# Attention in a two-layer diffusion block: the values of two pairs of heads in one PSUM tile, and separate slot rings for probabilities and their transposes

## The chip, the cores and the metric

The kernel runs on one core of a Trainium2 chip. The metric is the device time of one execution in microseconds. In the profiles the engines are PE (TensorE, matrix products; PEld are its weight loads), DVE (VectorE), ACT (ScalarE), POOL (GpSimd) and SP (SyncE, which issues the DMAs here). `L814` is line 814 of the kernel.

## What is computed

Two layers over 256 latent and 256 context tokens of width 1024. Each layer normalizes and modulates its input, multiplies it by one wide input matrix, runs three mixers on parts of the result (a short convolution, a Fourier mixing, an attention), gates and sums them, projects the sum, and ends with a squared-ReLU network. The part that matters here is the attention, with 8 query heads of 64 channels in 2 groups, each group sharing one key and value head:

```python
def gqa(q, k, v):
    b, lq = q.shape[:2]
    qg = q.reshape(b, lq, N_KV_HEADS, GQA_GROUP, HEAD_DIM)
    s = jnp.einsum('bqgrd,bkgd->bgrqk', qg, k).astype(jnp.float32) * (HEAD_DIM ** -0.5)
    p = jax.nn.softmax(s, axis=-1).astype(v.dtype)
    o = jnp.einsum('bgrqk,bkgd->bqgrd', p, v)
    return o.reshape(b, lq, ATTN_WIDTH)
```

Latent queries (256) read 512 keys, those of the latents and of the context. Context queries (256) read the 256 context keys, and only in layer 0. All data are float32.

## The kernel before

**Precision.** Large products are made of three passes: each operand is split into a high and a low part (`hilo`, L445, for activations; `split`, L356, for weights), and `fm` (L411) issues high x high (L434), low x high (L437) and high x low (L439). The weight parts are made by one ACT cast (L359) and one DVE subtraction (L360) for each 1024 columns.

**Attention.** A unit is one head, one block of 128 queries, one stream (s = 0 latents, s = 1 context). Layer 0 has 32 units, layer 1 has 16 (latents alone). They stand in the order stream, i, query block, head, where head is i and then i + 4; so two units that follow each other are the two groups' heads of one pair, and four units are both query blocks of that pair. One unit has three steps:

- `softmax` (L783): two PE products of scores into a PSUM tile (L789), DVE's maximum (L792), ACT's exponential into a slot of a ring (L795), DVE's reciprocal and scaling (L797, L798).
- `flip` (L801): 4 PE transposes of the probabilities (2 for context units) into a PSUM tile (L804), and an ACT copy into another slot (L806).
- `values` (L809), once for two units: for each key block one product for each of the two groups (L814), whose 64 output rows go to one half of the partitions of a PSUM tile of 128 columns; then `hilo` writes the high part (ACT, L446) and the low part (DVE, L447) into `qT`, where the queries of these heads have been read.

Both probabilities and transposed probabilities take their slots from one ring of 8 slots of 512 columns (`ar`, L775) in the order of the calls. PSUM tiles of the attention come from a pool of 3 (`aux`, L83), as do a few others.

**What sets the order.** `attend` (L777) is a generator: each `yield` is one step. `fm` calls `attn.tick()` (L442) after each block of the contraction, and `Side` (L336) takes 1.3 steps per tick in layer 0 and 0.8 in layer 1 (`AR`, L36). The ticks are those of the gate products, `gates` (L845) and the two branch products (L869, L870): 20 ticks in each of four rounds (L857). What is left is taken by `attn.drain()` (L875) before the third gate (`agL`). The loop at L824 takes, for each n, `softmax` of unit n, `flip` of unit n - 2 and, when n is even, `values` of units n - 4 and n - 3. `mods` works in the same manner for the modulation vectors of later stages (L241 to L333): DVE accumulations, then four small products with `ones` (L283), an ACT copy of their result (L288) and two transposes (L293). The tile framework then orders the instructions of each engine by a simulated time line; semaphores make each instruction wait for its inputs and for its slot.

**Names.** `gateL` and `agL` are the stages of the two gate parts, with a tile's name behind: `gateL_mm` are the PSUM tiles of the gate products, `gateL_aux` those of the attention, `qkvL_big` the ring and also `qT`, `qkvL_vt` the values, `gateL_mod` the modulation products. A product of L814 is float32 and leaves two records in the trace, so 8 of them are 16 records.

## Time and profile before

| | |
|---|---|
| median of 3 runs | 1155.12 us (1152.49 to 1155.44) |
| the profiled execution | 1154.74 us, its span 1153.0 us |
| mean granted PE clock | 0.997 of full speed |
| products of L814 in the trace | 320 records, first at 157.5 us, last at 903.7 us |
| transposes of L804 | 160, each of 128 columns |
| score products of L789 | 96 |
| gate stage of layer 0 | 127.6 to 281.6 us |
| gate stage of layer 1 | 821.4 to 905.5 us |

PE's matmul records overlap: one starts while the one before is still draining. So the time that an instruction takes on PE is read from the start of one record to the start of the next, not from its duration. The time line merges equal instructions that follow each other; its columns are start and length in us, engine, line, operation, output and inputs, shape, and their number.

### The profile page before, as it was taken

How to read it: one execution, taken by the hardware profiler on the slowest of the kernel's cores; microseconds unless marked ns; L12 is line 12 of the kernel's file. 1: busy time of each engine (PE TensorE's matmuls, PEld its weight loads, DVE VectorE, ACT ScalarE, POOL GpSimd, SP SyncE). 2: the span in 40 equal slices, each digit the busy share in tenths (PEclk: the TensorE clock that was granted, in tenths of full speed). 3: DMA queues.
4: the chain of work that ended last, by engine and by line, in shares of the span. 5: the costliest groups of instructions: out<-in, count | busy, mean ns of one | idle time of the engine just before them, and what ended most of it. 6: DMA issues, size and time to landing. Idle time of an engine off the chain costs nothing.

```text
span 1153.0 us, 17815 instructions
## 1 busy us (share of the span) xinstructions
PE 1130.3 (98%) x7083; PEld 982.5 (85%) x7083; DVE 781.7 (68%) x1446; ACT 504.6 (44%) x896; POOL 59.2 (5%) x57
## 2 busy tenths in 40 slices
PE   6899999999999999999999999999999999999998
PEld 5689987887787998888888888899999999988986
DVE  4677775567879785776655664778876567756754
ACT  4244444434332354144235135245665446754652
POOL 2102100000000100000000000033300000000000
PEclk9999999999999999999999999999999999999999
DMA  9923222224556254556456664625434365556553
GB/s 290 289 80 107 92 92 89 84 86 124 186 164 198 77 170 141 170 180 198 129 166 218 201 198 149 202 77 170 142 113 144 111 201 183 183 176 190 183 183 110
DMA packets 156764, 180.03 MB, mean 156 GB/s; under 512 B 5228, under 2 KB 126472, under 8 KB 156680
## 3 DMA queue, kind: packets, MB, share of 16 engines
q1 hardware_dynamic: 156680, 178.88, 49.0%
q8 instruction: 56, 0.92, 0.3%
q14 instruction: 28, 0.23, 0.1%
HBM read 177.81 MB, written 1.05 MB: 155 GB/s over the span
## 4 chain that ended last, share of the span: by engine, by line
PE 88%; DMA 4%; SPq 3%; DVE 3%; ACT 1%; issue 1%; POOL 0%; DVEq 0%; ACTq 0%
PE ffL_mm L434 12%; PE ffL_mm L437 12%; PE ffL_mm L439 12%; PE gateL_mm L434 5%; PE gateL_mm L437 5%; PE gateL_mm L439 5%; PE ffL_mm L1064 3%; PE ffL_mm L1062 3%; PE ffL_mm L1063 3%; PE agL_mm L434 2%; PE agL_mm L437 2%; PE agL_mm L439 2%; SPq L465 2%; PE gateL_aux L814 2%; PE woL_mm L437 2%; PE woL_mm L439 2%
## 5 line engine op out<-in xcount | busy, mean ns | idle before, releaser
L359 ACT CAST ffL_whi<-ffL_raw 128x1024 fp32r<-128x1024 f32 x128 | 134.4, 1052 | 218.2 <-PE ffL_mm L439 164.3
L360 DVE TENSOR_TENSOR ffL_wlo<-ffL_raw,ffL_whi 128x1024 fp32r<-128x1024 f32 x127 | 155.1, 1222 | 99.1 <-ACT ffL_whi L359 99.0
L434 PE MATMUL ffL_mm<-woL_big,ffL_whi 128*128 128x258 f32 (+2 forms) x544 | 171.1, 329 | 0.0
L437 PE MATMUL ffL_mm<-woL_big,ffL_wlo 128*128 128x258 f32 (+2 forms) x544 | 170.5, 327 | 0.0
L439 PE MATMUL ffL_mm<-woL_big,ffL_whi 128*128 128x258 f32 (+2 forms) x544 | 133.2, 328 | 0.0
L434 PEld LDWEIGHTS ffL_mm<-woL_big,ffL_whi 128*128 128x128 f32 x544 | 103.0, 190 | 10.2 <-issue 1.6
L437 PEld LDWEIGHTS ffL_mm<-woL_big,ffL_wlo 128*128 128x128 f32 x544 | 103.2, 190 | 8.9 <-issue 0.4
L326 DVE SCALAR_TENSOR_TENSOR ffL_acc<-ffL_modr,cs,ffL_acc 128x512 f32<-128x512 f32 x126 | 90.4, 746 | 25.7 <-DMA ffL_modr<-in_w_mod_dram 24.6
L434 PE MATMUL ffL_mm<-ffL_big,ffL_whi 128*128 128x512 f32 (+1 forms) x288 | 105.3, 368 | 0.0
L437 PE MATMUL ffL_mm<-ffL_big,ffL_wlo 128*128 128x512 f32 (+1 forms) x288 | 104.9, 367 | 0.0
L439 PEld LDWEIGHTS ffL_mm<-woL_big,ffL_whi 128*128 128x128 f32 x544 | 91.0, 190 | 8.7
L439 PE MATMUL ffL_mm<-ffL_big,ffL_whi 128*128 128x512 f32 (+1 forms) x288 | 85.1, 367 | 0.0
L434 PEld LDWEIGHTS ffL_mm<-ffL_big,ffL_whi 128*128 128x128 f32 x288 | 54.3, 189 | 10.6 <-issue 2.1
L437 PEld LDWEIGHTS ffL_mm<-ffL_big,ffL_wlo 128*128 128x128 f32 x288 | 54.3, 189 | 9.0 <-issue 0.4
L439 PEld LDWEIGHTS ffL_mm<-ffL_big,ffL_whi 128*128 128x128 f32 x288 | 53.2, 189 | 8.7
L360 DVE TENSOR_TENSOR gateL_wlo<-gateL_raw,gateL_whi 128x1024 fp32r<-128x1024 f32 x40 | 48.8, 1221 | 13.5 <-ACT gateL_whi L359 13.3
L359 ACT CAST gateL_whi<-gateL_raw 128x1024 fp32r<-128x1024 f32 x40 | 42.0, 1050 | 26.7 <-PE gateL_mm L439 20.7
L792 DVE TENSOR_REDUCE gateL_mx<-gateL_aux 128x1 f32<-128x512 f32 (+1 forms) x48 | 28.7, 599 | 34.5 <-PE gateL_aux L789 34.2
L434 PE MATMUL gateL_mm<-n1L_big,gateL_whi 128*128 128x512 f32 x128 | 50.8, 398 | 0.0
L437 PE MATMUL gateL_mm<-n1L_big,gateL_wlo 128*128 128x512 f32 x128 | 50.8, 397 | 0.0
L1062 PE MATMUL ffL_mm<-ffL_whi,ffL_big 128*128 128x512 f32 x128 | 49.9, 390 | 0.0
L1063 PE MATMUL ffL_mm<-ffL_wlo,ffL_big 128*128 128x512 f32 x128 | 49.8, 389 | 0.0
(335 smaller groups left out, 2658.5 us busy)
## 6 DMA issues: line engine op xcount, KB each, us to landing
ffL_raw<-in_w_ff_dram SPq DMA_DIRECT2D x64, 1024.0 KB, 5.4
ffL_modr<-in_w_mod_dram SPq DMA_DIRECT2D x53, 512.0 KB, 5.8
gateL_raw<-in_w_in_dram SPq DMA_DIRECT2D x16, 1024.0 KB, 6.8
init_big<-in_w_mod_dram SPq DMA_DIRECT2D x16, 512.0 KB, 7.8
agL_raw<-in_w_in_dram SPq DMA_DIRECT2D x8, 1024.0 KB, 5.0
woL_raw<-in_w_o_dram SPq DMA_DIRECT2D x8, 1024.0 KB
qkvL_raw<-in_w_in_dram SPq DMA_DIRECT2D x6, 1024.0 KB
agL_modr<-in_w_mod_dram SPq DMA_DIRECT2D x11, 512.0 KB, 4.2
```

Of the source, the lines that this page charges most:

```text
L326: v = V.scalar_tensor_tensor(a, r[:, kk, :], w, a, op0=ALU.mult, op1=ALU.add)
L359: a = A.copy(hi[:, :n], src)
L360: b = eng.tensor_tensor(lo[:, :n], src, hi[:, :n].bitcast(F32), op=ALU.subtract)
L434: m = PE.matmul(d, wh, rh, start=kt == first, stop=False)
L437: PE.matmul(d, wl, rh, start=False, stop=False)
L439: PE.matmul(d, wh, rl, start=False, stop=kt == final)
L465: nc.sync.dma_start(t[:, f, i], w_mod[0, :, c0 : c0 + P].rearrange("(k p) n -> p k n", p=P))
L792: V.reduce_max(mx, sc, axis=AX.X, negate=True)
L814: PE.matmul(yp[g * HD : (g + 1) * HD, :], vt[:, k0 + kk, g * HD : (g + 1) * HD], pts[g][:, kk, :], start=kk == 0, stop=kk == nk - 1,)
L1062: PE.matmul(bs[tt], hid[:, 0], wh, start=kk == 0, stop=False)
L1063: PE.matmul(bs[tt], hid[:, 0], wl, start=False, stop=False)
L1064: PE.matmul(bs[tt], hid[:, 1], wh, start=False, stop=kk == nk - 1)
```

## The change

The ring of 8 slots becomes two on the same memory: 3 slots for probabilities, 5 for transposed probabilities. `values` takes a group of two pairs (four units: both query blocks of heads i and i + 4), multiplies them one after the other into the two halves of one PSUM tile of 256 columns, and calls `hilo` once on 256 columns. It runs when the unit behind the group has been flipped, so once in four units; the number of products and their shapes stay. The generator has one `yield` fewer for each two pairs: 8 steps fewer in layer 0, 4 in layer 1.

```diff
     class Ring:
-        def __init__(self, n):
-            self.t, self.n, self.i = bigt([P, n, 4096 // n], F32), n, -1
+        def __init__(self, n, t=None, lo=0):
+            self.t = bigt([P, n, 4096 // n], F32) if t is None else t
+            self.n, self.lo, self.i = n, lo, -1
 
         def next(self):
             self.i += 1
-            return self.t[:, self.i % self.n, :]
+            return self.t[:, self.lo + self.i % self.n, :]
...
-        ar = Ring(8)
+        slots = bigt([P, 8, 512], F32)
+        ar, at = Ring(3, slots), Ring(5, slots, 3)
...
-                pt = ar.next().rearrange("p (k q) -> p k q", q=P)
+                pt = at.next().rearrange("p (k q) -> p k q", q=P)
...
-            def values(s, i, qt, pts):
-                k0, nk = (0, 4) if s == 0 else (2, 2)
-                yp = aux((P, P))
-                for kk in range(nk):
-                    for g in range(2):
-                        PE.matmul(
-                            yp[g * HD : (g + 1) * HD, :], vt[:, k0 + kk, g * HD : (g + 1) * HD],
-                            pts[g][:, kk, :], start=kk == 0, stop=kk == nk - 1,
-                        )
-                cs = slice(s * S + qt * P, s * S + (qt + 1) * P)
-                hilo(qT[:, i, cs], qT[:, i + 4, cs], yp)
+            def values(group):
+
+                yp = aux((P, 2, P))
+                for n, ((s, i, qt), pts) in enumerate(group):
+                    k0, nk = (0, 4) if s == 0 else (2, 2)
+                    for kk in range(nk):
+                        for g in range(2):
+                            PE.matmul(
+                                yp[g * HD : (g + 1) * HD, n, :],
+                                vt[:, k0 + kk, g * HD : (g + 1) * HD],
+                                pts[g][:, kk, :], start=kk == 0, stop=kk == nk - 1,
+                            )
+                (s, i, qt), _ = group[0]
+                cs = slice(s * S, (s + 1) * S)
+                hilo(qT[:, i, cs], qT[:, i + 4, cs], yp.rearrange("p n q -> p (n q)"))
...
-                v = f - 2
-                if v >= 0 and v % 2 == 0:
-                    s, i, qt, _ = units[v]
-                    values(s, i, qt, (pts.pop(v), pts.pop(v + 1)))
+                v = f - 4
+                if v >= 0 and v % 4 == 0:
+                    values([(units[u][:3], (pts.pop(u), pts.pop(u + 1))) for u in (v, v + 2)])
                     yield
```

The lines of the file move by 3 up to the ring and by 4 to 7 behind it: the gate products L434, L437, L439 become L437, L440, L442; scores L789 become L793, transposes L804 become L808, value products L814 become L820.

How the instructions stand on PE is shown at three places. The first is the first values in layer 0, on PE, before the change (units 0 to 3, with a gate product's last part ahead and a further part between them):

```order
L439 MATMUL gateL_mm_1748<-convL_big_674,gateL_whi_1749 128x512
L814 MATMUL gateL_aux_1654<-qkvL_big_1450,qkvL_vt_895 64x128 x8
L434 MATMUL gateL_mm_1792<-convL_big_674,gateL_whi_1749 128x512
...
L789 MATMUL gateL_aux_1698<-qkvL_kT_894,qkvL_big_893 128x512 x2
L804 MATMUL gateL_aux_1714<-ident,qkvL_big_1450 128x128 x4
L814 MATMUL gateL_aux_1729<-qkvL_big_1450,qkvL_vt_895 64x128 x8
L437 MATMUL gateL_mm_1843<-n1L_big_188,gateL_wlo_1845 128x512
```

And the same values on PE after it:

```order
L437 MATMUL gateL_mm_1845<-n1L_big_188,gateL_whi_1846 128x512
L440 MATMUL gateL_mm_1845<-n1L_big_188,gateL_wlo_1847 128x512
L808 MATMUL gateL_aux_1697<-ident,qkvL_big_1450 128x128 x4
L820 MATMUL gateL_aux_1709<-qkvL_big_1450,qkvL_vt_895 64x128 x16
L793 MATMUL gateL_aux_1737<-qkvL_kT_894,qkvL_big_893 128x512 x2
L442 MATMUL gateL_mm_1845<-n1L_big_189,gateL_whi_1846 128x512
```

The two runs of 8 have become one of 16, which stands behind the transposes of unit 4. Over the whole of layer 0 the products of L814 stand in 17 unbroken runs before and those of L820 in 8 after; in layer 1 in 10 before and 5 after. In every case the transposes of unit n - 3 stand ahead of the scores of unit n, and the values of a group ahead of the transposes of the unit that takes its first slot next.

The second place is the end of the gate stage of layer 0 on PE, before the change, from the last gate product (L439 on the branch input) to the first product of the next stage (`agL_mm`):

```order
L439 MATMUL gateL_mm_2840<-convL_big_674,gateL_whi_2822 128x512
L804 MATMUL gateL_aux_2602<-ident,qkvL_big_1450 128x128 x2
L789 MATMUL gateL_aux_2606<-qkvL_kT_894,qkvL_big_893 128x256 x2
L283 MATMUL gateL_mod_2709<-gateL_acc_2210,ones 32x256 x2
...
L804 MATMUL gateL_aux_2710<-ident,qkvL_big_1450 128x128 x2
L814 MATMUL gateL_aux_2720<-qkvL_big_1450,qkvL_vt_895 64x128
L283 MATMUL gateL_mod_2709<-gateL_acc_2211,ones 32x256 x2
L814 MATMUL gateL_aux_2720<-qkvL_big_1450,qkvL_vt_895 64x128 x3
L293 MATMUL gateL_aux_2791<-ident,gateL_scr_2767 128x128 x2
L434 MATMUL agL_mm_2864<-n1L_big_188,agL_whi_2866 128x512
```

And the same end after it (12 gate products are left out behind the values):

```order
L442 MATMUL gateL_mm_2797<-convL_big_674,gateL_whi_2798 128x512
L808 MATMUL gateL_aux_2614<-ident,qkvL_big_1450 128x128 x2
L808 MATMUL gateL_aux_2624<-ident,qkvL_big_1450 128x128 x2
L820 MATMUL gateL_aux_2628<-qkvL_big_1450,qkvL_vt_895 64x128 x8
L437 MATMUL gateL_mm_2815<-convL_big_674,gateL_whi_2798 128x512
...
L286 MATMUL gateL_mod_2696<-gateL_acc_2233,ones 32x256 x2
L286 MATMUL gateL_mod_2696<-gateL_acc_2234,ones 32x256 x2
L296 MATMUL gateL_aux_2767<-ident,gateL_scr_2743 128x128 x2
L437 MATMUL agL_mm_2840<-n1L_big_188,agL_whi_2842 128x512
```

The last four units of the attention stood behind all gate products and now stand ahead of the last 12. The four modulation products (L286) now stand next to the transposes of their result (L296), with nothing between.

The third place is the end of the attention in layer 1 on PE after the change: the last group is split in 9 and 7 products, with 13 gate products between.

```order
L808 MATMUL gateL_aux_8303<-ident,qkvL_big_7534 128x128 x4
L820 MATMUL gateL_aux_8319<-qkvL_big_7534,qkvL_vt_7154 64x128 x9
L440 MATMUL gateL_mm_8403<-ffL_big_6713,gateL_wlo_8434 128x256
...
L440 MATMUL gateL_mm_8467<-ffL_big_6713,gateL_wlo_8470 128x256
L820 MATMUL gateL_aux_8319<-qkvL_big_7534,qkvL_vt_7154 64x128 x7
```

Before the change the last two pairs stood there in four runs (1, 7, 1 and 7 products), so the 10 runs of that layer have become 5. Outside the gate stages, and three small modulation products just behind that of layer 0, the order on PE, DVE and ACT is as before; SP issues one modulation load two places earlier.

## The prediction

> **What bounds the kernel now.** I read the page's head and its chain first, then the two gate stages as windows, since all of the attention lies in them. All sums are made against the profiled execution, 1154.74 us with a span of 1153.0 us; the median of the runs shown is 0.4 us above it. Those runs lie 2.95 us apart, 0.26%, so 0.3% (3.5 us) is about what a measurement of this kernel can tell from no change.
>
> ```profile
> span 1153.0 us, 17815 instructions
> PE 1130.3 (98%) x7083; PEld 982.5 (85%) x7083; DVE 781.7 (68%) x1446; ACT 504.6 (44%) x896; POOL 59.2 (5%) x57
> PE 88%; DMA 4%; SPq 3%; DVE 3%; ACT 1%; issue 1%; POOL 0%; DVEq 0%; ACTq 0%
> ```
>
> PE is on the chain for 88% of the span. The windows give the stretch from the first gate product to the third gate, for layer 0 and layer 1; the columns are the window, its length, then busy time and number of PE, PEld, DVE, ACT and POOL, the PE clock, the DMA share and rate.
>
> ```profile
> 127.60:281.60 154.00, 153.12 (x867) 121.64 (x865) 98.37 (x196) 70.90 (x157) 1.01 (x1) 1.00 0.31 97
> 821.40:905.50 84.10, 84.10 (x721) 79.56 (x720) 58.77 (x117) 50.24 (x101) 3.53 (x3) 1.00 0.41 131
> ```
>
> PE is busy for 153.12 of 154.00 us and for all of 84.10 us, at full clock; DVE has 55 us to spare in layer 0 and ACT 83 us. So fewer instructions on ACT and DVE are worth nothing by themselves here. The change leaves the number of PE's products as it is. What can move the time is how long PE takes for the same products in another order, and the few waits that it has. Both are read from the time line, from start to start.
>
> **What a run of value products costs PE.** Layer 0, a run of 16 records between gate products:
>
> ```profile
> 156.92 0.63 PE L439 MATMUL gateL_mm<-convL_big,gateL_whi 128*128 128x512 f32 x2
> 157.48 1.09 PE L814 MATMUL gateL_aux<-qkvL_big,qkvL_vt 128*64 128x128 f32 x16
> 158.51 0.50 PE L434 MATMUL gateL_mm<-convL_big,gateL_whi 128*128 128x512 f32 x1
> 158.84 0.39 PE L437 MATMUL gateL_mm<-convL_big,gateL_wlo 128*128 128x512 f32 x1
> 159.07 0.63 PE L789 MATMUL gateL_aux<-qkvL_kT,qkvL_big 128*128 128x512 f32 x2
> ```
>
> A gate product in the middle of others takes 0.23 us (158.84 to 159.07). The two ahead of the run take 0.56 instead of 0.46, and the one behind it 0.33 instead of 0.23: entering and leaving cost 0.10 each, 0.20 together. The run itself takes 1.03 us. A run of 8 records, with two products per group instead of four:
>
> ```profile
> 255.06 0.40 PE L434 MATMUL gateL_mm<-n1L_big,gateL_whi 128*128 128x512 f32 x1
> 255.39 0.66 PE L814 MATMUL gateL_aux<-qkvL_big,qkvL_vt 128*64 128x128 f32 x8
> 255.98 0.50 PE L437 MATMUL gateL_mm<-n1L_big,gateL_wlo 128*128 128x512 f32 x1
> 256.31 0.39 PE L434 MATMUL gateL_mm<-n1L_big,gateL_whi 128*128 128x512 f32 x1
> ```
>
> It takes 0.59 us, and its entry and exit cost 0.10 each again. So 8 more records cost 0.44, and 8 alone 0.59: a run has a fixed part of 0.15 us inside beside the 0.20 at its ends. In layer 1 the gate products have 256 columns and take 0.12 us:
>
> ```profile
> 849.89 0.36 PE L434 MATMUL gateL_mm<-ffL_big,gateL_whi 128*128 128x256 f32 x1
> 850.19 1.09 PE L814 MATMUL gateL_aux<-qkvL_big,qkvL_vt 128*64 128x128 f32 x16
> 851.21 0.38 PE L437 MATMUL gateL_mm<-ffL_big,gateL_wlo 128*128 128x256 f32 x1
> 851.43 0.40 PE L439 MATMUL gateL_mm<-ffL_big,gateL_whi 128*128 128x256 f32 x2
> 851.67 0.28 PE L434 MATMUL gateL_mm<-ffL_big,gateL_whi 128*128 128x256 f32 x1
> ```
>
> Here the entry costs 0.30 - 0.12 = 0.18 and the exit 0.22 - 0.12 = 0.10; with the 0.15 inside a run has 0.43 us of its own.
>
> Whether the fixed part belongs to a run, or to each accumulation that is begun, decides whether two pairs side by side save it. Layer 1 has a pair whose 16 records are split by gate products, within one pair of accumulations:
>
> ```profile
> 896.93 0.43 PE L814 MATMUL gateL_aux<-qkvL_big,qkvL_vt 128*64 128x128 f32 x2
> 897.29 0.38 PE L437 MATMUL gateL_mm<-ffL_big,gateL_wlo 128*128 128x256 f32 x1
> ...
> 897.84 1.09 PE L814 MATMUL gateL_aux<-qkvL_big,qkvL_vt 128*64 128x128 f32 x14
> 898.86 0.66 PE L804 MATMUL gateL_aux<-ident,qkvL_big 128*128 128x128 f32 x4
> ```
>
> The two parts take 0.36 and 1.02, 1.38 us where the unsplit run takes 1.03. Splitting costs 0.35 us inside, with the same accumulations. So the fixed part goes by runs. By this row it could be 0.35 rather than 0.15; I take 0.15, from the two whole lengths, and keep 0.35 as the far end.
>
> A rule of the Trainium skill speaks against this whole part. "TensorE: Matmul & The Clock Gate", section on the back-to-back issue gap, gives a sustained spacing of about 81 ns per matmul at 128 columns, the same for each one. By it the products would cost the same in any grouping, and this term would be zero. The rows differ from it: 2 records in 0.36 us, 16 in 1.03.
>
> **The change, part by part.** *Merged runs.* The order of PE shows 17 runs before and 8 after in layer 0, 10 and 5 in layer 1. Nine runs fewer at 0.20 + 0.15 = 0.35 are 3.2 us; five at 0.40, between 0.35 and the 0.43 above, are 2.0 us. PE waits for nothing there, so all of it is on the path: **5.2 us less**. (Ten of the 17 begin behind transposes, where the transposes' own exit and the run's entry can't be told apart; I price them as the others.) If two pairs side by side saved nothing inside, only the ends would go: 9 x 0.20 + 5 x 0.28 = 3.2 us. With 0.35 inside it would be 9 x 0.55 + 5 x 0.63 = 8.1 us.
>
> *The end of the attention in layer 0.* Before, the last units stand behind all gate products, with nothing beside them:
>
> ```profile
> 276.80 0.51 PE L789 MATMUL gateL_aux<-qkvL_kT,qkvL_big 128*128 128x256 f32 x2
> 277.14 0.38 PE L804 MATMUL gateL_aux<-ident,qkvL_big 128*128 128x128 f32 x2
> 278.37 0.41 PE L804 MATMUL gateL_aux<-ident,qkvL_big 128*128 128x128 f32 x2 [0.85 <-DVE qkvL_big L798]
> ...
> 279.30 0.44 PE L804 MATMUL gateL_aux<-ident,qkvL_big 128*128 128x128 f32 x2
> ...
> 280.03 0.63 PE L283 MATMUL gateL_mod<-gateL_acc,ones 128*32 128x256 f32 x4
> 280.58 0.65 PE L814 MATMUL gateL_aux<-qkvL_big,qkvL_vt 128*64 128x128 f32 x6
> 281.16 0.44 PE L293 MATMUL gateL_aux<-ident,gateL_scr 128*128 128x128 f32 x2
> 281.62 0.50 PE L434 MATMUL agL_mm<-n1L_big,agL_whi 128*128 128x512 f32 x1
> ```
>
> Two transposes alone take 0.13 to 0.15 us, so from 277.14 to 278.37 PE loses about 1.1 us to a softmax that is not done. After the change eight fewer steps at 1.3 per tick end the attention six ticks earlier, and eight gate products (1.8 us) and two transposes stand between the last scores and their transposes. The last softmax before, from the end of its scores (277.1) to its transposes (279.30), takes 2.2 us; 2.0 of that is now covered, and the 1.1 us go. What is late next is the modulation: its products were followed by 6 value records (0.58 us) that hid the ACT copy of their result; now the transposes stand next to them:
>
> ```profile
> 280.70 0.37 ACT L288 COPY gateL_scr<-gateL_mod 128x256 f32<-128x256 f32 x1 [0.50 <-PE gateL_mod L283]
> ```
>
> From the products' end (280.58) over the copy to 281.16 are 0.58 us, which now stand open: 0.6 us back. Net **0.5 us less**; bounds 1.1 less, and 1.5 more if the last softmax is as exposed as before and the values wait for the last two copies too.
>
> *Fewer writes of the result.* ACT's cast and DVE's subtraction go from 24 each on 128 columns to 12 on 256.
>
> ```profile
> L446 ACT CAST qkvL_big<-gateL_aux x24: 266/267/284, 158.6 to 904.0; 128x128 fp32r<-128x128 f32 x24
> L446 ACT CAST qkvL_scr<-qkvL_big x10: 402/407/418, 108.9 to 828.7; 128x256 fp32r<-128x256 f32 x10
> ```
>
> ACT: 24 x 0.267 = 6.4 us become 12 x about 0.41 = 4.9 (the nearest row of 256 columns reads SBUF, not PSUM). DVE saves about as much. PE's work hides both: worth 0. Uncovered it would be 1.5 us.
>
> *The rings.* Three slots for probabilities and five for transposes have no slack: the exponential of unit n needs the transposes of unit n - 3 done, and a copy needs the values of the group whose slot it takes. PE issues both ahead of the scores and the transposes that these instructions wait for anyway, so the waits end before others do: 0. If one did hold, ACT would stand with the weight casts queued behind it, and the gate products behind those.
>
> Behind the gate stages the order is the same, each load is issued when its buffer comes free, and nothing is tied to absolute time; the gain carries through to the end. Sum: 5.2 + 0.5 = 5.7 us less, 1154.74 - 5.7 = **1149.0 us**.
>
> **The rivals.** *Only the ends are saved.* Inside a run the second pair could start anew in its own columns; then 3.2 + 0.5 = 3.7 us go: 1151.0 us. The split pair speaks against it, though it shows a split and not a joint. The Trainium skill, "TensorEngine Tiling (Array Packing)", section on key properties, says that a change of the tiling mode drains TensorE, which is a cost of the two ends alone; by it the sum is this rival's. Its rows here are the 0.10 at each end; the 1.38 against 1.03 shows more than that.
>
> *The gain is eaten at the ends of the attention.* In both layers the last values stand directly behind the last transposes. If the end of layer 0 costs the 1.5 us of its bound, and that of layer 1 another 1 us, 5.2 - 2.5 = 2.7 us remain: 1152.0 us. Against it: the 8 gate products ahead, and in layer 1 the split with 13 products (1.6 us) between.
>
> *Slower: values wait for the copies.* A group needs four copies at once. If the copy of its last unit is late, PE stands, and with it the gate products. Waits for a copy so far:
>
> ```profile
>   ACT qkvL_big L806: 1.0, 3
> ```
>
> That is 1.0 us in three waits over all value products. It would decide from about 0.8 us a group: 12 x 0.8 = 9.6, less the 5.7 saved, 3.9 us slower, 1158.6 us. Against it: in the new order, summed with the spacings above, ten of twelve groups start 2.4 to 6.3 us behind the transposes that they need last, most 3 us or more, and before it was 2.9 to 6.1 for the first 13 pairs of layer 0.
>
> *No cost of a run at all*, as by the skill's even spacing: 0.5 us from the end of layer 0, 1154.2 us. The rows quoted speak against it.
>
> **How the numbers follow.** Forecast 1149.0 us, chance 0.58. Only the ends, 1151.0: 0.17, of which half falls below 1151.3, the bound of 0.3%. Eaten at the ends, 1152.0: 0.13. Waits for copies: 0.07. No cost of a run: 0.05. So faster 0.58 + 0.09 = 0.67, the same 0.08 + 0.13 + 0.05 = 0.26, slower 0.07. The forecast's own range takes the far end of the inside part in full only with the end of layer 0 at its best, 1154.74 - 8.1 - 1.1 = 1145.5; I take 1146.5, since both at once are unlikely. Upward the range takes in the two cases after it, up to 3.2 - 1.5 = 1.7 us saved: 1153.0. Left out are waits for copies, no cost of a run, and the outermost corner, some 0.15.
>
> **What would show it.** The time line should have runs of 32 records (16 for context units), a run of 32 in about 1.9 us (1.03 + 2 x 0.44); 2.06 would mean that only the ends are saved. The stretch from the first gate product to the third gate should be 150.3 us in layer 0 (154.0 - 3.2 - 0.5) and 82.1 in layer 1 (84.1 - 2.0), and all behind it as long as before. The idle 0.85 us on L798 should be gone, and about 0.5 us idle stand ahead of the modulation's transposes. ACT should show 12 casts of 256 columns. Waits of L820 for L810 well above 1 us in total would make me wrong, as would weight casts that wait in ACT behind the rings.

## The result and the profile after

The changed kernel takes 1148.13 us (median of 6 runs, 1147.48 to 1149.57); the kernel before, run beside it, 1154.89 us (median of 6). The ratio is 0.9948, with a 95% interval of 0.9938 to 0.9958: 0.52% faster, 6.0 us; the two medians themselves lie 6.8 us apart. Predicted were 5.7 us less. The profiled execution took 1147.6 us. Of the runs of the experiments below, one of e6_two_writes_rate (5639.62 us) and one of e7_context_of_8 (1591.98 us) were slow; the ratios leave these two out, the medians count them.

The page's head and chain after the change:

```profile
span 1145.7 us, 17784 instructions
PE 1123.6 (98%) x7083; PEld 980.9 (86%) x7083; DVE 779.8 (68%) x1434; ACT 503.2 (44%) x884; POOL 59.1 (5%) x57
PE 90%; SPq 3%; DMA 3%; DVE 2%; ACT 1%; POOL 0%; issue 0%; DVEq 0%; ACTq 0%
```

PE has as many instructions as before, is busy for 6.7 us less, and still bounds the kernel. ACT and DVE have 12 instructions fewer each. The windows of the two gate stages, from the first gate product to the third gate as before:

```profile
126.02:276.27 150.25, 149.35 (x867) 121.07 (x865) 96.75 (x189) 70.00 (x150) 1.01 (x1) 1.00 0.34 102
816.46:898.84 82.38, 82.38 (x723) 79.30 (x722) 57.66 (x113) 49.83 (x97) 3.57 (x3) 1.00 0.41 128
```

Layer 0's stage is 154.00 - 150.25 = 3.75 us shorter. Its busy time is 153.12 - 149.35 = 3.77 us less, and its idle time is the same (0.88 before, 0.90 after). Layer 1's stage has no idle time in either kernel and is 1.7 us shorter by the rounded edges of the window of before, 1.9 by the starts of the records (821.39 to 905.66 before, 84.27).

The products of L820 in PE's time line of layer 0, a run between transposes and scores and one behind a gate product:

```profile
165.10 0.60 PE L808 MATMUL gateL_aux<-ident,qkvL_big 128*128 128x128 f32 x4
165.63 1.97 PE L820 MATMUL gateL_aux<-qkvL_big,qkvL_vt 128*64 128x128 f32 x32
167.53 0.72 PE L793 MATMUL gateL_aux<-qkvL_kT,qkvL_big 128*128 128x512 f32 x2
...
198.40 0.40 PE L442 MATMUL gateL_mm<-convL_big,gateL_whi 128*128 128x512 f32 x1
198.73 1.97 PE L820 MATMUL gateL_aux<-qkvL_big,qkvL_vt 128*64 128x128 f32 x32
200.62 0.73 PE L793 MATMUL gateL_aux<-qkvL_kT,qkvL_big 128*128 128x512 f32 x2
```

32 records take 1.90 and 1.89 us, where two runs of 16 took 2 x 1.03. The gate product ahead of the second run takes 0.33 instead of 0.23 us: the entry of 0.10 is still paid, once for two pairs.

The end of layer 0's stage, on PE and then on ACT:

```profile
273.98 0.39 PE L442 MATMUL gateL_mm<-convL_big,gateL_whi 128*128 128x512 f32 x1
274.30 0.64 PE L286 MATMUL gateL_mod<-gateL_acc,ones 128*32 128x256 f32 x8
275.77 0.44 PE L296 MATMUL gateL_aux<-ident,gateL_scr 128*128 128x128 f32 x2 [0.84 <-ACT gateL_scr L291]
276.27 0.50 PE L437 MATMUL agL_mm<-n1L_big,agL_whi 128*128 128x512 f32 x1
```

```profile
274.40 1.05 ACT L362 CAST agL_whi<-agL_raw 128x1024 fp32r<-128x1024 f32 x1 [2.61 <-PE gateL_mm L442]
275.36 0.36 ACT L291 COPY gateL_scr<-gateL_mod 128x256 f32<-128x256 f32 x1
```

The idle 0.85 us on the last softmax is gone. In its place PE waits 0.84 us for the copy of the modulation's result. That copy is 0.36 us long, but it began only at 275.36, at the end of a weight cast of 1.05 us that ACT had begun at 274.40, beside the modulation's products.

Behind layer 0's stage one wait of PE grew, for a modulation's accumulation in the feed-forward stage; the first row is of the waits before, the second of those after (columns: total, times, longest, in us):

```profile
PE ffL_mod L283 <- DVE ffL_acc L326: 0.6, 1, 0.6
```

```profile
PE ffL_mod L286 <- DVE ffL_acc L329: 1.1, 1, 1.1
```

Between the two stages this gives 0.4 us back (539.77 us before, 540.19 after). The two spans differ by 7.3 us: 3.7 and 1.9 from the stages, less 0.4, about 0.5 behind layer 1, and 1.6 from the start, where the first gate product came at 126.02 us instead of 127.64. Of the eleven other kernels below, which all have the same start, ten have it at 127.4 to 128.0 and one (e10) at 126.53. The granted clock, the share of PE's full speed that the profile lists as granted, tells them apart: from 45 to 60 us it is 1.00 in the executions of the changed kernel and of e10, and 0.89 in the other eleven. So the 1.6 us are a difference of single executions and no gain. Nor are the 0.5 us behind layer 1: that stretch takes 247.31 us in the execution of before and 246.80 in that of e1, which has the same order. What the traces show of the gain lies between: from the first gate product of layer 0 to the third gate of layer 1 it is (905.66 - 127.64) - (898.84 - 126.02) = 5.2 us, within the interval of the ratio (4.9 to 7.2 us).

### The profile page after: what moved, and what is told of

Read it like the earlier page. It is cut to its first block, busy times and chain, and to the rows that moved or that the text cites. A ratio compares the mean times of both kernels' runs of the same rounds, so it can differ in the third digit from the quotient of the medians.

```text
span 1145.7 us, 17784 instructions
## 1 busy us (share of the span) xinstructions
PE 1123.6 (98%) x7083; PEld 980.9 (86%) x7083; DVE 779.8 (68%) x1434; ACT 503.2 (44%) x884; POOL 59.1 (5%) x57
## 3 DMA queue, kind: packets, MB, share of 16 engines
HBM read 177.81 MB, written 1.05 MB: 156 GB/s over the span
## 4 chain that ended last, share of the span: by engine, by line
PE 90%; SPq 3%; DMA 3%; DVE 2%; ACT 1%; POOL 0%; issue 0%; DVEq 0%; ACTq 0%
PE ffL_mm L437 12%; PE ffL_mm L440 12%; PE ffL_mm L442 12%; PE gateL_mm L437 5%; PE gateL_mm L440 5%; PE gateL_mm L442 5%; PE agL_mm L440 3%; PE agL_mm L437 3%; PE agL_mm L442 3%; PE ffL_mm L1070 3%; PE ffL_mm L1071 3%; PE ffL_mm L1069 3%; SPq L468 2%; PE woL_mm L440 2%; PE woL_mm L442 2%; PE woL_mm L437 2%
## 5 line engine op out<-in xcount | busy, mean ns | idle before, releaser
L437 PE MATMUL ffL_mm<-woL_big,ffL_whi 128*128 128x258 f32 (+2 forms) x544 | 171.1, 329 | 0.0
L440 PE MATMUL ffL_mm<-woL_big,ffL_wlo 128*128 128x258 f32 (+2 forms) x544 | 170.5, 327 | 0.0
L442 PE MATMUL ffL_mm<-woL_big,ffL_whi 128*128 128x258 f32 (+2 forms) x544 | 133.2, 328 | 0.0
L437 PEld LDWEIGHTS ffL_mm<-woL_big,ffL_whi 128*128 128x128 f32 x544 | 103.0, 190 | 10.2 <-issue 1.6
L440 PEld LDWEIGHTS ffL_mm<-woL_big,ffL_wlo 128*128 128x128 f32 x544 | 103.1, 190 | 8.9 <-issue 0.4
L437 PE MATMUL ffL_mm<-ffL_big,ffL_whi 128*128 128x512 f32 (+1 forms) x288 | 105.3, 368 | 0.0
L440 PE MATMUL ffL_mm<-ffL_big,ffL_wlo 128*128 128x512 f32 (+1 forms) x288 | 104.9, 367 | 0.0
L442 PEld LDWEIGHTS ffL_mm<-woL_big,ffL_whi 128*128 128x128 f32 x544 | 91.0, 190 | 8.7
L442 PE MATMUL ffL_mm<-ffL_big,ffL_whi 128*128 128x512 f32 (+1 forms) x288 | 85.0, 367 | 0.0
L437 PEld LDWEIGHTS ffL_mm<-ffL_big,ffL_whi 128*128 128x128 f32 x288 | 54.3, 189 | 10.6 <-issue 2.1
L440 PEld LDWEIGHTS ffL_mm<-ffL_big,ffL_wlo 128*128 128x128 f32 x288 | 54.3, 189 | 9.0 <-issue 0.4
L442 PEld LDWEIGHTS ffL_mm<-ffL_big,ffL_whi 128*128 128x128 f32 x288 | 53.1, 189 | 8.7
L437 PE MATMUL gateL_mm<-n1L_big,gateL_whi 128*128 128x512 f32 x128 | 50.6, 397 | 0.0
L440 PE MATMUL gateL_mm<-n1L_big,gateL_wlo 128*128 128x512 f32 x128 | 50.3, 393 | 0.0
L1069 PE MATMUL ffL_mm<-ffL_whi,ffL_big 128*128 128x512 f32 x128 | 49.9, 390 | 0.0
L1071 PE MATMUL ffL_mm<-ffL_whi,ffL_big 128*128 128x512 f32 x128 | 49.8, 389 | 0.0
```

Source lines behind the costliest of these rows:

```text
L437: m = PE.matmul(d, wh, rh, start=kt == first, stop=False)
L440: PE.matmul(d, wl, rh, start=False, stop=False)
L442: PE.matmul(d, wh, rl, start=False, stop=kt == final)
L1069: PE.matmul(bs[tt], hid[:, 0], wh, start=kk == 0, stop=False)
L1071: PE.matmul(bs[tt], hid[:, 1], wh, start=False, stop=kk == nk - 1)
```

## The experiments

Every run stands beside runs of the kernel before on the same chip (medians of 1153.62 to 1154.34 us there), and the ratio is to these. The table gives the ratio with its interval, and from one profiled execution each the starts of PE's records: layer 0's stage, the stretch from layer 0's first gate product to layer 1's (which contains that stage and all up to the next attention), and layer 1's stage. All in us.

| kernel | median | ratio to before (95%) | runs of values, layers 0 / 1 | layer 0 | to layer 1 | layer 1 |
|---|---|---|---|---|---|---|
| before | 1154.89 | 1 | 17 / 10 | 153.98 | 693.75 | 84.27 |
| after | 1148.13 | 0.9948 (0.9938 to 0.9958) | 8 / 5 | 150.25 | 690.44 | 82.38 |
| e1_rings | 1154.10 | 0.9997 (0.9988 to 1.0006) | 17 / 10 | 153.99 | 693.60 | 84.27 |
| e2_two_writes | 1154.37 | 0.9999 (0.9990 to 1.0008) | 8 / 5 | 155.47 | 695.89 | 82.45 |
| e3_split_runs | 1152.16 | 0.9979 (0.9969 to 0.9990) | 18 / 6 | 153.27 | 693.10 | 82.90 |
| e4_steps | 1148.12 | 0.9943 (0.9930 to 0.9955) | 9 / 5 | 149.73 | 689.14 | 82.37 |
| e5_before_rate | 1162.59 | 1.0071 (1.0058 to 1.0083) | 16 / 10 | 159.70 | 702.14 | 84.28 |
| e6_two_writes_rate | 1152.38 | 0.9984 (0.9975 to 0.9993) | 9 / 5 | 153.55 | 694.89 | 82.46 |
| e7_context_of_8 | 1153.39 | 0.9993 (0.9984 to 1.0001) | 7 / 5 | 152.57 | 695.38 | 82.37 |
| e8_after_rate | 1150.62 | 0.9968 (0.9956 to 0.9980) | 9 / 5 | 152.08 | 691.62 | 82.36 |
| e9_two_writes_steps | 1148.03 | 0.9953 (0.9939 to 0.9968) | 9 / 5 | 149.75 | 689.29 | 82.46 |
| e10_steps_slower | 1149.00 | 0.9969 (0.9956 to 0.9982) | 10 / 5 | 148.66 | 690.47 | 82.37 |
| e11_steps_slowest | 1150.49 | 0.9972 (0.9961 to 0.9983) | 8 / 5 | 145.47 | 692.14 | 82.37 |

The theory: the gain comes from PE entering and leaving the value products less often. The rivals: it comes from the rings, from the fewer writes on ACT and DVE, or from another place of the attention's end (8 steps fewer at the same pace).

### The rings alone

The kernel before with the two rings and nothing else:

```diff
-        ar = Ring(8)
+        slots = bigt([P, 8, 512], F32)
+        ar, at = Ring(3, slots), Ring(5, slots, 3)
...
-                pt = ar.next().rearrange("p (k q) -> p k q", q=P)
+                pt = at.next().rearrange("p (k q) -> p k q", q=P)
```

> Kernel before with the two rings (3 and 5 slots) alone; the values stay in pairs with one write each. The order on PE is that of before, 17 runs of value products in layer 0 and 10 in layer 1. If the gain comes from the merged runs: as before, ratio 1.000, gate stages 154.0 and 84.2 us. If the rings gave some of it: faster than before, up to 6 us.

No difference: 0.9997, and both stages as before to 0.01 us. The rings do not make the gain and do not cost anything.

### One run of products, two writes

The changed kernel with two writes of 128 columns behind one run of products:

```diff
-                (s, i, qt), _ = group[0]
-                cs = slice(s * S, (s + 1) * S)
-                hilo(qT[:, i, cs], qT[:, i + 4, cs], yp.rearrange("p n q -> p (n q)"))
+                for n, ((s, i, qt), _) in enumerate(group):
+                    cs = slice(s * S + qt * P, s * S + (qt + 1) * P)
+                    hilo(qT[:, i, cs], qT[:, i + 4, cs], yp[:, n, :])
```

> Kernel after, but each pair's result is written by its own cast and subtraction of 128 columns (24 of each, as before); the products of two pairs stay in one run. 8 and 5 runs of value products, as after; but the end of the attention in layer 0 stands behind all gate products again (6 transposes, 8 value products and the modulation products in a row). If merged runs are the cause: layer 1 stage 82.4 us as after; layer 0 150.3 plus 1 to 2.5 us for the exposed end; total 1149 to 1151 us. If fewer writes are the cause: both stages as before, 154.0 and 84.2 us, total 1155 us.

Layer 1 came out as expected (82.45), layer 0 not: 155.47, and the whole gain was given back. PE's time line at the end of that stage:

```profile
269.80 0.48 PE L793 MATMUL gateL_aux<-qkvL_kT,qkvL_big 128*128 128x256 f32 x2
271.58 0.50 PE L437 MATMUL gateL_mm<-convL_big,gateL_whi 128*128 128x512 f32 x1 [1.29 <-DVE gateL_scr L862]
...
277.01 0.44 PE L808 MATMUL gateL_aux<-ident,qkvL_big 128*128 128x128 f32 x2 [0.52 <-ACT qkvL_big L810]
279.11 0.41 PE L808 MATMUL gateL_aux<-ident,qkvL_big 128*128 128x128 f32 x2 [1.66 <-DVE qkvL_big L802]
279.45 1.97 PE L820 MATMUL gateL_aux<-qkvL_big,qkvL_vt 128*64 128x128 f32 x16
281.35 1.08 PE L286 MATMUL gateL_mod<-gateL_acc,ones 128*32 128x256 f32 x8
```

The order has moved: the last units stand behind all gate products again, and PE waits 1.29 us for DVE's gating (L862), 0.52 for a copy and 1.66 for a softmax. The last run of 16 takes 1.90 us from start to start instead of 1.03. The window of this run shows why; the granted clock is the third number from the end:

```profile
279.10:281.35 2.25, 2.24 (x18) 1.76 (x18) 2.14 (x4) 0.37 (x1) 0.00 (x0) 0.57 0.03 7
```

The clock was 0.57 here and 0.63 up to 283.40 us, and 1.00 ahead of this and behind it. By these two windows 0.43 x 2.25 + 0.37 x 2.05 = 1.7 us went to the clock. So behind the waits PE was slower as well as late. Whether the second write does this itself, or only the place of the end, was open at this point; e9 below answers it.

### One write, two runs of products

The changed kernel with one PSUM tile and one write for each group, its two pairs multiplied one unit apart:

```diff
+                if n0 == 0:
+                    return
                 (s, i, qt), _ = group[0]
...
-                if v >= 0 and v % 4 == 0:
-                    values([(units[u][:3], (pts.pop(u), pts.pop(u + 1))) for u in (v, v + 2)])
+                if v >= 0 and v % 4 < 2:
+                    if v % 4 == 0:
+                        yp = aux((P, 2, P))
+                    u = v + v % 4
+                    values([(units[u][:3], (pts.pop(u), pts.pop(u + 1)))], v % 4, yp)
                     yield
```

> Kernel after, with one tile and one write for two pairs, but the second pair's products issued one unit later than the first's. Layer 0 has 18 runs of value products (after: 8), layer 1 has 6 (after: 5), since there the order puts most pairs side by side again. If a run costs 0.35 us of its own: layer 0 150.3 + 10 x 0.35 = 153.8 us, layer 1 82.4 + 0.35 = 82.8, total about 1152 us. If it is the single write or the earlier slots: as after, 1148 us.

As expected: 153.27 and 82.90. In its time line two score products stand between the two pairs of a group:

```profile
167.10 1.09 PE L819 MATMUL gateL_aux<-qkvL_big,qkvL_vt 128*64 128x128 f32 x16
168.13 0.73 PE L793 MATMUL gateL_aux<-qkvL_kT,qkvL_big 128*128 128x512 f32 x2
168.79 1.09 PE L819 MATMUL gateL_aux<-qkvL_big,qkvL_vt 128*64 128x128 f32 x16
```

The pairs take 1.03 us each again, and the scores between them 0.66 where two gate-sized products take 0.46 (0.10 for leaving, 0.10 for entering). The window of layer 0 of this kernel:

```profile
127.49:280.76 153.27, 153.27 (x867) 121.92 (x865) 97.90 (x188) 68.83 (x149) 1.01 (x1) 1.00 0.33 100
```

PE waits for nothing here, and still needs 153.27 us. ACT and DVE have the fewer, larger writes (ACT 68.83 us busy), and these alone shorten nothing in layer 0: without the 0.88 us of idle time that the kernel before has, it would need 153.12.

### The steps

The changed kernel with an empty step behind each group, which restores the old number of steps:

```diff
                     values([(units[u][:3], (pts.pop(u), pts.pop(u + 1))) for u in (v, v + 2)])
                     yield
+                    yield
```

> Kernel after with a second, empty step behind each group of values, so that the attention takes as many steps as before and ends later in layer 0; 9 and 5 runs of value products. If merged runs are the cause: layer 0 150.3 + 0.35 for the one run more, and 0 to 1 us for the end, layer 1 82.4, total 1148.5 to 1149.5 us. If the fewer steps are the cause: 1153 to 1155 us.

The gain stays: 0.9943. So fewer steps are not its cause. The window of its layer 0:

```profile
127.54:277.27 149.73, 149.71 (x868) 121.38 (x866) 96.27 (x188) 69.17 (x149) 1.01 (x1) 1.00 0.33 103
```

Like e3, this kernel has next to no idle time on PE in the stage, so the two can be compared directly: nine runs fewer take 153.27 - 149.71 = 3.56 us less, **0.40 us per run** (predicted 0.35). The end of its stage:

```profile
275.67 0.63 PE L286 MATMUL gateL_mod<-gateL_acc,ones 128*32 128x256 f32 x4
276.23 0.66 PE L820 MATMUL gateL_aux<-qkvL_big,qkvL_vt 128*64 128x128 f32 x8
276.81 0.44 PE L296 MATMUL gateL_aux<-ident,gateL_scr 128*128 128x128 f32 x2
277.27 0.50 PE L437 MATMUL agL_mm<-n1L_big,agL_whi 128*128 128x512 f32 x1
```

Eight value records stand between the modulation's products and its transposes and cover the copy on which the changed kernel waits 0.84 us.

### A faster pace

If an uncovered end is what costs, more steps per tick should end the attention earlier and cover it. Three kernels try this: the kernel before at 1.6 steps per tick in layer 0, the version with two writes at 1.5, and the changed kernel at 1.5. The edit of the first, which in the other two has 1.5:

```diff
-AR = [1.3, 0.8]
+AR = [1.6, 0.8]
```

> Kernel before with 1.6 attention steps per tick in layer 0 instead of 1.3: the attention ends among the gate products, the pairs stay single. 16 runs of value products in layer 0 (before: 17) and 10 in layer 1. If the merged runs carry the gain: layer 0 about 153.5 us (0.35 for one run, 1.1 for the wait that is now covered, about 1 back for the last copy and the modulation), total 1153 to 1154.5 us. If an early end of the attention carries it: 150 us and 1150.5 us.

> The kernel with merged runs and two writes of 128 columns per group, with 1.5 steps per tick in layer 0 instead of 1.3, so that its attention ends among the gate products. 9 and 5 runs. If two writes cost nothing and the loss of that kernel at 1.3 came from the uncovered end alone: layer 0 149.7 to 150.6 us, layer 1 82.4, total 1148 to 1149 us. If the second write itself costs: layer 0 above 152 us.

> Kernel after with 1.5 steps per tick in layer 0: 9 and 5 runs, the modulation products split by gate products. The idle time ahead of the modulation's transposes should go: layer 0 149.5 to 150.0 us against 150.25 after, total 1147.5 to 1148.5 us. If pace matters beyond the order's end: outside 149 to 151 us.

Layer 1 came out as expected in all three. Layer 0 was missed in all three: 159.70, 153.55 and 152.08 us. By their expectations the second of these was to mean that the second write costs, which e9 below answers, and the third that the pace matters beyond the end. For the kernel before, PE's time line shows in the middle and at the end of the stage:

```profile
206.00 0.51 PE L789 MATMUL gateL_aux<-qkvL_kT,qkvL_big 128*128 128x256 f32 x2 [0.47 <-DVE qkvL_big L447]
...
281.39 0.65 PE L814 MATMUL gateL_aux<-qkvL_big,qkvL_vt 128*64 128x128 f32 x6 [0.82 <-ACT qkvL_big L806]
284.95 1.38 PE L283 MATMUL gateL_mod<-gateL_acc,ones 128*32 128x256 f32 x8 [2.91 <-DVE gateL_acc L326]
```

The last transposes and values still stand at the end of PE's order, though more steps are taken per tick, and now the modulation's accumulation on DVE is 2.91 us late. Behind this wait the clock fell again: it was 0.73 from 284.90 to 287.30 us and 0.50 from there to 290. In the middle, at 203 to 211 us, scores, transposes, modulation products and values of several units stand together without gate products between, and wait for each other's DVE and ACT work. The version with two writes has such a wait of 0.63 us at the same place:

```profile
204.56 0.48 PE L793 MATMUL gateL_aux<-qkvL_kT,qkvL_big 128*128 128x256 f32 x2 [0.63 <-DVE qkvL_big L450]
```

In the changed kernel at 1.5 the waits that the profile names in this stage are two at its end:

```profile
274.38 0.50 PE L437 MATMUL gateL_mm<-convL_big,gateL_whi 128*128 128x512 f32 x1 [0.25 <-DVE gateL_scr L862]
...
279.58 0.44 PE L296 MATMUL gateL_aux<-ident,gateL_scr 128*128 128x128 f32 x2 [0.85 <-ACT gateL_scr L291]
```

PE's idle time in the stage is 1.2 us by the window, 0.3 more than at 1.3; the other 1.5 of the 1.83 us are spread over the stage. By the starts of the records, this idle time included, scores, transposes and values take 1.2 us more in all and the modulation's products and transposes 0.5; why is open.

### Context units in groups of eight

e4 with the context units in groups of four pairs, their transposes in half slots:

```diff
-                pt = at.next().rearrange("p (k q) -> p k q", q=P)
+                if nk == 4:
+                    pt = at.next()
+                else:
+                    j, half[0] = half[0] % 10, half[0] + 1
+                    pt = slots[:, 3 + j // 2, (j % 2) * 256 : (j % 2 + 1) * 256]
+                pt = pt.rearrange("p (k q) -> p k q", q=P)
...
-                v = f - 4
-                if v >= 0 and v % 4 == 0:
+                g = 4 if f <= 16 else 8
+                v = f - g
+                if v >= 0 and v % g == 0:
...
```

The PSUM tile and the write, which grow with the group, and the empty step are left out here. In this kernel the first context unit's transposes overwrite those of the last latent unit before its values are formed, so the values of one latent pair come from other probabilities; the work is the same.

> Kernel after with the empty second step behind each group, and with the context units of layer 0 in groups of eight (their transposes have half the columns, so ten half slots hold them): 7 and 5 runs. If a run has 0.35 us of its own: layer 0 149.7 - 2 x 0.35 = 149.0 us, or up to 149.9 where the last transposes stand directly ahead of the last run; total 1147.5 to 1148.5 us. If the fixed part does not go on shrinking with the number of runs: 149.7 us or more.

Missed: 152.57. There is one run fewer than in the changed kernel, but the end waits for the modulation's accumulation, as in e5:

```profile
274.10 1.97 PE L827 MATMUL gateL_aux<-qkvL_big,qkvL_vt 128*64 128x128 f32 x32
278.14 0.90 PE L286 MATMUL gateL_mod<-gateL_acc,ones 128*32 128x256 f32 x4 [2.07 <-DVE gateL_acc L329]
```

The time by itself is what was expected if the fixed part did not shrink further, but it does not decide this: PE is idle for 2.54 us in the stage, and from 278 to 280 us the clock is 0.59, which is 0.8 us. PE's busy time of 150.03 us, less this 0.8, is 149.2, 0.5 us below that of e4, which has two runs more; 0.7 were expected of the two. The low clock (0.53 from 278 to 285 us) goes on into the next stage.

### Two writes, with the empty step

e2 and e4 together: two writes, and the empty step behind each group.

> The changed kernel with two writes of 128 columns for each group (one run of products still) and the empty step behind each group, at the old rate of 1.3 steps per tick. It tells apart why two writes with one run gave the gain in layer 0 back: theory A, the end of the attention of that version stood behind all gate products, and its second write costs PE nothing itself; theory B, the second cast and subtraction delay what is queued behind them on ACT and DVE, wherever the attention ends. The order still ends layer 0 with transposes, 4 values, modulation products and 4 values in a row, but 12 gate products stand ahead of these. Layer 1 of both: 82.4 us. A: layer 0 149.8 to 151.0 us (149.73 with one write and the empty step, and up to 1.3 for the two writes at the end), time 1148 to 1149.5. B: layer 0 above 152 us, time 1151 to 1154, with waits of PE for products of DVE's subtraction or for gate tiles in the middle of the stage.

Theory A holds: 149.75 us, 0.02 from e4 with one write, and 0.9953. The order of the end:

```profile
274.92 0.66 PE L820 MATMUL gateL_aux<-qkvL_big,qkvL_vt 128*64 128x128 f32 x8
275.51 0.64 PE L286 MATMUL gateL_mod<-gateL_acc,ones 128*32 128x256 f32 x8
276.08 0.81 PE L820 MATMUL gateL_aux<-qkvL_big,qkvL_vt 128*64 128x128 f32 x8
276.82 0.44 PE L296 MATMUL gateL_aux<-ident,gateL_scr 128*128 128x128 f32 x2
```

So the second cast and subtraction of a group cost PE nothing that these traces can tell (0.02 us in layer 0, 0.09 in layer 1). What differs is the order: in e2 all the last units stand behind the gate products, and here 12 gate products (2.8 us) stand behind the last scores, and cover the softmax. Against e2 the empty step, which issues nothing, is worth 155.47 - 149.75 = 5.7 us: 4.0 us less idle time of PE (0.38 instead of 4.41), and the 1.7 us that the low clock took in e2.

### A slower pace

e4 at 1.2 and at 1.1 steps per tick in layer 0.

> The changed kernel with the empty step behind each group, and 1.2 steps of the attention per tick in layer 0 instead of 1.3. A faster pace (1.5) made layer 0 longer by 1.8 us. Theory A: a faster pace bunches the steps of the attention at the ends of the rounds, so waits appear; a slower one spreads them. By the order the last four value products stand among gate products (4, then 1 behind ten products, then 3 behind four) and the transposes of the modulation have products between. Layer 0 149.2 to 150.2 us (149.73 at 1.3; one more run of values costs 0.35, the covered modulation gives some back), time 1147.5 to 1148.6. Theory B: any move of the end costs some us, since the transfers and the vector work that it meets there are other ones: layer 0 151 to 153 us, time 1149.5 to 1151.5. Layer 1 82.4 us by both.

> As the run before it with 1.1 steps per tick in layer 0. Now the modulation's products and its transposes come long before the end, and the last transposes and the last 8 value products stand among and behind gate products as one run. Eight unbroken runs of values as in the changed kernel, no wait for the modulation's copy (0.84 us there). Theory A (a slower pace spreads the steps): layer 0 149.0 to 149.9 us, time 1147.2 to 1148.3; only the wait for the last softmax and its copy can stand open, up to 1 us. Theory B (any move costs): layer 0 151 to 153 us, time 1149.5 to 1151.5. Layer 1 82.4 us by both.

Neither theory gave both numbers right. The stages are short (148.66 and 145.47), but that mark is no longer the attention's end: products of the third gate now stand ahead of the last transposes and values (in e11 from 273.41 us on, the last values at 286.28). So the stretch to layer 1 is compared instead: 690.47 and 692.14 against 689.14 at 1.3. The times, 1149.0 and 1150.49 us, are no better than at 1.3. In e11 PE's longest wait up to layer 1 is a modulation's, in the next stage:

```profile
328.03 1.20 PE L286 MATMUL agL_mod<-agL_acc,ones 128*32 128x256 f32 x8
331.64 0.69 PE L296 MATMUL agL_aux<-ident,agL_scr 128*128 128x128 f32 x2 [2.41 <-ACT agL_scr L291]
```

This one wait is 2.41 us, and the clock of 0.65 from 331.6 to 336.0 us took another 1.5; together they are more than the 3.0 us by which e11 is longer than e4, so all else in e11 is about 1 us shorter. The wait lies in the same chain as before, accumulation, products, copy, transposes, now in the stage that follows. In e10, which is 1.3 us longer than e4, the same wait is 0.88 us.

## Why the prediction was right

**Merged runs: right, in mechanism and nearly in size.** The two parts, 0.20 at the ends and 0.15 inside in layer 0, were to give 0.35 us a run; e3 against e4 measured 0.40. For nine runs 3.2 us were predicted; PE's busy time fell by 3.77, and e3 against e4 gives 3.56. Layer 1's five runs were to give 2.0 and gave 1.89, 0.38 each. The run of 32 records was to take 1.9 us and takes 1.90. "Only the ends are saved" wanted 2.06 and a slower time, so it falls; "no cost of a run at all" falls with e3. The rule of the Trainium skill that was weighed there ("TensorE: Matmul & The Clock Gate", back-to-back issue gap, an even spacing of about 81 ns) does not give the price of these runs: 32 records take 59 ns each, 16 take 64 ns, 8 take 74 ns, and the ends come on top.

The single records show where the part inside lies. The products of the two groups run side by side: their records start in pairs, 0.109 us from pair to pair (55 ns a record). Only the first step is longer, 0.160, and from the last pair to the next instruction it is 0.209: 0.05 + 0.10 make the 0.15 us, so this part too belongs to the borders of a run. The 0.35 us that the prediction kept as its far end come from the odd split: the last product of a run of 1 or 7 products has no partner and takes as long as two would. A product alone takes 0.36 us (2 records, at 896.93 before), two side by side 0.37 (4 records, at 258.73 in e3).

All traces together say the same as e3 and e4. PE's busy time from layer 0's first gate product to layer 1's, less what a clock below 1.00 took, is 690.0 to 690.6 us in the four kernels with 16 to 18 runs in layer 0 and 685.4 to 688.7 us in the nine with 7 to 10. Within the nine it does not follow the number alone: at nine runs e4 and e9 have 686.7 and 686.2, e8 and e6 have 687.8 and 688.7, and why is open.

**The end of layer 0: a net zero instead of 0.5 less.** The idle 0.85 us at the softmax went as predicted. What came in its place, the copy of the modulation's result, was named and sized at 0.6 us; it took more because of a weight cast that stood ahead of it on ACT. From the modulation products' end (274.30 + 0.57, as the same eight take from start to start in e9) to 275.77 are 0.90 us. The step "from the products' end over the copy to the transposes", 0.58 us, counted on an ACT that was free.

**Fewer writes: worth 0 by themselves, shown.** e9 differs from e4 in this alone and is as fast, within 0.1 us in both gate stages. At the changed kernel's own pace the single write did matter, through the order: with two (e2) the end stood behind all gate products and the gain was gone.

**The rings: worth 0, shown** by e1.

**Waits for copies: none on PE.** The answer on the waits ahead of the value products of the changed kernel, over PE and PEld:

```profile
  issue: 2.3, 9
  ACT qkvL_big L799: 0.4, 1
```

No copy (L810) is among them, where before there was 1.0 us. But these rows, and the 1.0 us that the prediction went by, are idle time of the weight loads (PEld), which overlap PE's products. For PE alone the profile shows no idle time ahead of the value products in either kernel. So the prediction read idle weight loads as waits of PE. The rival that was to make the kernel slower did not come up.

**"The gain carries through": nearly.** 0.4 us of layer 0's gain is lost at a modulation's accumulation before layer 1. The sum of 5.7 us stands beside 3.73 + 1.89 = 5.6 us in the two stages and 6.0 us between the runs. That the sum is so close is in part luck: layer 0's runs gave 0.6 us more than was priced (3.77 instead of 3.2 of busy time), and its end 0.5 us less, and the two cancel.

**What the prediction took too lightly** is how much its small second term depends on the order that comes out. It bounded the end of layer 0 by 1.1 us less and 1.5 more. e2, e5 and e8 show that the same products in about the same number of runs can need 1.8 to 5.7 us more in that stage in another order. The changed kernel got an end that costs no more than the one before. The expectations of e5 to e8 failed on this same point: they took an earlier end as a covered one. What stands last in PE's order is not set by the number of steps alone, and the modulation's chain, which is not part of the attention, is late there in six of these kernels (the changed kernel, e2, and e5 to e8), the softmax in three (the kernel before, e1 and e2).

No version was clearly faster than the changed kernel. e4 and e9 (0.9943 and 0.9953) are as fast within their intervals; that they reach layer 1 1.1 to 1.3 us sooner is too little for these runs to tell apart.

## What to carry to other kernels

When PE is the bound and small products of another shape stand among large ones, price them by runs, and read from the time line the fixed part of a run at its ends and inside: here 0.35 to 0.40 us for each run. Grouping then pays though it gains nothing on the other engines, as long as the order of the stage's end does not give it back, as in e2. So take such a gain in a stage whose end is uncovered only with a look at the order of that end: a change that costs no engine anything can move it by several us. Compare an experiment with another that has no idle time in the stage and the same granted clock; then the difference is the cost itself.

## What the runs showed that was not expected

- An empty step of a generator, no instruction, changes layer 0 by 5.7 us (e2 against e9) or by 0.5 us (after against e4), through the order and what followed from it: idle time of PE, and in e2 the low clock.
- A long wait of PE cost more than its own length here. Between 100 and 1140 us of the thirteen traces the granted clock is below 1.00 in four, once in each: e2, e5, e7 and e11. It falls there at the end of the longest wait of PE or within 1.1 us behind it (1.66, 2.91, 2.07 and 2.41 us). In the other nine the longest wait of PE is 1.25 to 1.54 us.
- The cast of 256 columns out of PSUM is shorter than the same cast out of SBUF, which had served as the estimate (0.41 us). The answer to a query of L449 after the change, with the shortest, median and longest duration in ns:

```profile
L449 ACT CAST qkvL_big<-gateL_aux x12: 372/373/376, 167.6 to 891.2; 128x256 fp32r<-128x256 f32 x12
L449 ACT CAST qkvL_scr<-qkvL_big x10: 402/406/419, 107.3 to 823.8; 128x256 fp32r<-128x256 f32 x10
```
